# A projection of 2048 rows as eight units of seven products, with the sums of its operand's rows made on GpSimd

## The chip, the cores and the metric

One core of a Trainium2 chip runs the kernel. TensorE (PE) does matmuls, VectorE (DVE), ScalarE (ACT) and GpSimd (POOL) the elementwise work, and SyncE (SP) issues nearly all DMAs, in order, on one queue. The metric is the device time of one execution, in microseconds. Before the change it is 2262.46 us, the median of three runs (2262.41, 2262.46 and 2264.36).

## The reference

A decoder block on x of 1024 rows (time) and 1024 columns, in float32. Two mixers read the same normalised rows; a gated sum of their projections goes through an output projection and a squared-ReLU MLP. The part around the change:

```
o_a: 1024 x 512    (attention: four head slots of 128)
o_r: 1024 x 2048   (retention: four heads of 512; per head a recurrence over
                    chunks of 128 rows, group norm, scale and shift, times silu(gr))
y   = sigmoid(gate_a) * (o_a @ w_proj_a) + sigmoid(gate_b) * (o_r @ w_proj_b)
x   = x + y @ w_out
xn2 = rmsnorm(x, norm2_g)
x   = x + square(relu(xn2 @ w_up)) @ w_down
```

w_proj_b has 2048 rows and 1024 columns.

## The kernel before

**Numbers and layouts.** Each float32 operand is split into a high part h and a low part l (`split`, L318: ACT makes h in L319, DVE makes l = x - h in L320), and each product of two tiles is three matmuls, h h, h l and l h (`Pipe.group`). Operands are kept transposed: 128 columns of x or y on the partitions, the 1024 rows along the free axis, in two halves of 512 (`halves`, `cs`).

**Weights.** `Weights` (L38) holds the list of all weight loads and splits in the order of use. A raw buffer of 128 x 1024 is loaded by SP as soon as the buffer is free, and split into one of a few numbered buffers as soon as the products that read that buffer are done (`free`, `pump`). `add` (L61 on) takes a plain weight, `add_units` (L95) a unit of seven products: from two raw buffers it makes the pieces A, B and C (1024 columns each) and D (512), with four sums of 512 columns on DVE (L121) between them.

**Seven products.** `product` (L369) multiplies a 2 x 2 block matrix with seven products in place of eight: a unit is 256 output columns (f = 0, 1) by two halves of rows (lo, hi) over 1024 terms, and each product N1 to N7 has four terms of 128, so 12 matmuls. Its operands are sums and differences of the four quarters of the transposed input, made once and read by all units. Three PSUM banks and some copies put the products together, and `result(j, f, cs, src)` gets each of the four results. `in` (690 to 1002 us), `up` and `down` are made so in the kernel before; retention's output projection isn't.

**The order on the engines.** The order of the matmuls is written out by hand (`Pipe.step`, with functions set by `pipe.at` to come some steps later, such as retention's transposes), and a scheduler orders the other engines by the program's order and the waits. SP's DMAs form one queue, in which a DMA that waits holds up all behind it.

**Retention** (1002 to 1300 us). Per head h (4) and chunk c (8): values, scores, output and state on PE, the norm on DVE with the power on POOL (L853), then `turn_o` (L871): four transposes, scale and shift on ACT, the multiplication by the gate sr on DVE (L882), and one store of 4 x 128 rows by 128 columns to on_d in DRAM (L883).

**Projection of A** (1300 to 1360 us). For each block d of 128 output columns (8) and each half: 12 matmuls into a bank `ms`, then DVE multiplies by the gate sigmoid(gate_a) that was loaded from sg_d (L941), and the result is stored to pa_d. Beside it run the loads of the first half of o_r (`load_o`, 8 tiles of 128 x 1024 from on_d, each split). The first four go to buffers that are free already, the last four to buffers that are made when retention has ended.

**Projection of B** (1360 to 1534 us, L954 to L991). Two passes over w_proj_b's rows, first heads 0 and 1, then heads 2 and 3. Each pass is 8 blocks d x 2 halves of 8 terms x 3 = 24 matmuls (`project`, L959): 768 in all. In the first pass ACT copies the bank and SP stores it to pb_d, and the second half of o_r is loaded and split. In the second pass the sum of the first (pb_d), the gate (sg_d) and pa_d are loaded one step ahead, and DVE adds (L989), multiplies (L990), adds (L991), and the result is split into X, the operand of the next stage.

**Out** (1534 to 1640 us): y @ w_out in two halves of columns, 8 row tiles each, the residual, the norm and the transposes into the operands of `up` (OP7, six or seven sums of rows made on DVE).

## Time and profile before

| what | value |
|---|---|
| median of three runs | 2262.46 us |
| profiled execution, span | 2267.2 us |
| retention | 1002 to 1300.5 us |
| projection of A | 1301 to 1360.16 us |
| projection of B | 1360.16 to 1534.4 us |
| out | 1534.4 to 1640 us |
| HBM read, written | 200.48 MB, 92.37 MB |

The profiled execution is one of its own; its span, from the first to the last instruction on the core, stands in the second row. Times of stages are read from the first and last matmul or DVE instruction of the stage in the timeline. In the views, a row of windows has the stretch, its length, the busy time of each engine with its count of instructions, the granted clock of TensorE, the mean busy share of the 16 DMA engines and what they moved in GB/s. A row of groups has the line, engine, operation, output and inputs, shape and count, then the busy time in us, the mean ns of one, and the idle time before them with what ended it. A row of the timeline has start, duration and instruction, with what it waited for in brackets. A row of DMA issues has destination and source, queue, count, KB of each and the median us from issue to landing.

### The profile page before, as it was taken

Reading aid. Unit: us, or ns where it says so; the run is one execution under the profiler, and the core shown is the slowest. Engines: PE = TensorE matmul, PEld = TensorE weight load, DVE = VectorE, ACT = ScalarE, POOL = GpSimd, SP = SyncE. Lnnn points to the kernel's source line nnn. Section 1 sums busy time; section 2 is a strip of 40 time slices with the busy share of each in tenths; the row PEclk is TensorE's granted clock in tenths of the full one; section 3 lists DMA queues with packets and bytes.
Section 4 is the critical chain, followed back from the end, with each engine's and each line's share of the span. In section 5 each row is a group of like instructions: output and inputs, shape, how many; then the busy total and the mean of one; then the engine's idle time right before and its main releaser. Section 6 shows DMA issues by size and latency. Waiting matters only on the chain. (4 is left out here: it accounts for less than half of the span.)

```text
span 2267.2 us, 30458 instructions
## 1 busy us (share of the span) xinstructions
PE 2233.0 (98%) x10868; PEld 1912.0 (84%) x10868; DVE 1285.7 (57%) x2468; ACT 1014.0 (45%) x2294; POOL 344.3 (15%) x372
## 2 busy tenths in 40 slices
PE   8999999999999999999999999999999999899999
PEld 7999999998888888888888878888788888788777
DVE  6444545455544445558676753253855556687874
ACT  5444434345433333345555633112555545654542
POOL 1111111110000000000000000000000000587873
PEclk9999999999999999999999999999999999999999
DMA  4313232323233333363433385554345556645432
GB/s 148 98 52 105 65 91 85 94 85 99 82 109 106 110 109 111 113 186 117 122 117 97 121 267 183 155 184 153 107 127 151 151 152 199 218 153 179 169 129 102
DMA packets 227146, 294.85 MB, mean 130 GB/s; under 512 B 14129, under 2 KB 157873, under 8 KB 226994
## 3 DMA queue, kind: packets, MB, share of 16 engines
q1 hardware_dynamic: 226994, 292.91, 41.1%
q8 instruction: 85, 1.39, 0.3%
q14 instruction: 67, 0.55, 0.1%
HBM read 200.48 MB, written 92.37 MB: 129 GB/s over the span
## 5 line engine op out<-in xcount | busy, mean ns | idle before, releaser
L320 DVE TENSOR_TENSOR wl<-raw,wh 128x1024 fp32r<-128x1024 f32 (+2 forms) x274 | 300.4, 1099 | 398.0 <-ACT wh L319 396.9
L223 PE MATMUL mm<-wh,xh 128*128 128x384 f32 (+1 forms) x1226 | 482.0, 393 | 0.6 <-DVE Y L1203 0.5
L223 PE MATMUL mm<-wh,xl 128*128 128x384 f32 (+1 forms) x1226 | 438.8, 358 | 2.2 <-DVE xl L320 2.2
L223 PE MATMUL mm<-wl,xh 128*128 128x384 f32 (+1 forms) x1226 | 437.7, 357 | 0.0
L319 ACT ACTIVATE wh<-raw 128x1024 fp32r<-128x1024 f32 (+2 forms) x274 | 260.0, 951 | 358.2 <-PE ms L223 102.2
L223 PE MATMUL mm<-xl,wh 128*128 128x512 f32 x848 | 309.3, 389 | 1.7 <-DVE xl L320 1.7
L223 PE MATMUL mm<-xh,wh 128*128 128x512 f32 x848 | 309.7, 390 | 0.9 <-ACT ms L388 0.9
L223 PE MATMUL mm<-xh,wl 128*128 128x512 f32 x720 | 280.1, 389 | 0.0
L223 PEld LDWEIGHTS mm<-wh,xl 128*128 128x128 f32 x1226 | 230.9, 188 | 22.2 <-DVE xl L320 3.0
L223 PEld LDWEIGHTS mm<-wh,xh 128*128 128x128 f32 x1226 | 231.8, 189 | 20.0 <-DVE Y L1203 1.3
L223 PEld LDWEIGHTS mm<-wl,xh 128*128 128x128 f32 x1226 | 232.7, 190 | 16.6
L223 PE MATMUL ms<-xh,wh 128*128 128x512 f32 x604 | 239.3, 396 | 5.0 <-DVE s L941 3.5
L223 PE MATMUL ms<-xl,wh 128*128 128x512 f32 x604 | 235.8, 390 | 0.7 <-DVE xl L320 0.7
L223 PE MATMUL ms<-xh,wl 128*128 128x512 f32 x604 | 235.9, 391 | 0.0
L223 PEld LDWEIGHTS mm<-xl,wh 128*128 128x128 f32 x848 | 159.2, 188 | 34.9 <-DVE xl L320 2.1
L223 PEld LDWEIGHTS mm<-xh,wh 128*128 128x128 f32 x848 | 159.2, 188 | 34.2 <-ACT ms L388 1.3
L223 PEld LDWEIGHTS mm<-xh,wl 128*128 128x128 f32 x720 | 135.1, 188 | 28.1
L853 POOL TENSOR_TENSOR st<-st,half 128x1 f32<-128x1 f32 x32 | 25.8, 808 | 765.3 <-DVE st L852 765.3
L223 PEld LDWEIGHTS ms<-xh,wh 128*128 128x128 f32 x604 | 113.9, 189 | 31.2 <-issue 2.3
L223 PEld LDWEIGHTS ms<-xh,wl 128*128 128x128 f32 x604 | 113.7, 188 | 23.9
L223 PEld LDWEIGHTS ms<-xl,wh 128*128 128x128 f32 x604 | 113.9, 189 | 23.5 <-DVE xl L320 1.0
L333 POOL TENSOR_TENSOR ssa<-ssa,half 128x2 f32<-128x2 f32 x96 | 66.5, 693 | 427.9 <-DVE ssa L332 411.2
(296 smaller groups left out, 3605.1 us busy)
## 6 DMA issues: line engine op xcount, KB each, us to landing
raw<-in_w_att SPq DMA_DIRECT2D x48, 384.0 KB, 3.9
raw<-in_w_up SPq DMA_DIRECT2D x32, 512.0 KB, 3.9
h_d<-s SPq DMA_DIRECT2D x64, 256.0 KB, 4.5
raw<-in_w_down SPq DMA_DIRECT2D x32, 512.0 KB, 4.1
xh<-h_d SPq DMA_DIRECT2D x11, 896.0 KB, 4.5
xl<-h_d SPq DMA_DIRECT2D x10, 896.0 KB, 4.6
r<-h_d SPq DMA_DIRECT2D x10, 896.0 KB, 5.6
sg_d<-sg SPq DMA_DIRECT2D x32, 256.0 KB, 2.0
```

Source lines behind the costliest of these rows:

```text
L223: self.nc.tensor.matmul(ps, x, y, start=start, stop=stop, skip_group_check=not first)
L319: nc.scalar.activation(dst_h, src, AF.Copy)
L320: nc.vector.tensor_tensor(dst_l, src, dst_h.bitcast(F), op=OP.subtract)
L333: nc.gpsimd.tensor_tensor(dst, dst, half[:, :w], op=OP.pow)
L853: nc.gpsimd.tensor_tensor(st[:, 9:10], st[:, 8:9], half[:, 0:1], op=OP.pow)
```

## The change

Projection of B becomes eight units of seven products. w_proj_b is handed to `add_units` in quarters; units j = 0 to 3 are heads 0 and 1 (rows 0 to 1023 of w_proj_b), j = 4 to 7 heads 2 and 3. 8 units x 7 products x 12 matmuls are 672 matmuls.

The sums of rows that the seven products read are made in retention: a chunk c < 4 keeps its onT in one of five buffers and stores it; chunk c + 4 makes, on GpSimd, four sums and differences of 128 x 256 with it and stores ten row blocks (three DMAs) in place of four (one). on_d has 14 blocks for a head and a pair of chunks where it had 8. `load_sum` loads an operand's half, 128 x 1024, and splits it: 28 loads in place of 16, 12 of them beside the projection of A (after retention has made room, but for the first four, N5 and N7, whose buffers are there), four behind it, 12 in units 1 to 3, each operand of heads 2 and 3 one product after the last use of its buffer.

The gate is multiplied in both halves of the rows of w_proj_b: for each result the gate and an old sum (pa_d, or pb_d for j > 3) are loaded two results ahead, into rings of three buffers. DVE multiplies gate and product, which frees the bank; GpSimd adds the old sum (DVE for j = 7); for j < 4 the sum is stored to pb_d, for j > 3 it is split into the operand of out. The (f = 0, lo) results of j > 3 go through a small DRAM tile yl_d, since their place is still read. The buffers that w_out's weights are split into, and the places of out's and up's operands, change with it.

The diff, without places that only follow from it:

```diff
@@ -289,7 +289,8 @@
     sg_d = dram.tile([2, KT, P, S], F, name="sg_d")
     rqk_d = dram.tile([RH, 2, 2, P, S], F, name="rqk_d")
     sr_d = dram.tile([NF, P, S], F, name="sr_d")
-    on_d = dram.tile([NF, P, S], F, name="on_d")
+    on_d = dram.tile([RH, 14, P, 512], F, name="on_d")
+    yl_d = dram.tile([4, P, 512], F, name="yl_d")
     pa_d = dram.tile([KT, P, S], F, name="pa_d")
     pb_d = dram.tile([KT, P, S], F, name="pb_d")
     v_d = dram.tile([HEADS, S, DH], F, name="v_d")
@@ -352,12 +353,10 @@
             W.add(a["w_rv"][h, u])
     for d in range(KT):
         W.add(a["w_pa"][d])
-    for c in range(2):
-        for d in range(KT):
-            W.add(a["w_pb"][c, d])
+    W.add_units("pb", [a["w_pb_q"][j] for j in range(8)])
     for nb in range(2):
         for u in range(4):
-            W.add(a["w_out"][nb, u], (4, 5, 2, 3)[u] if nb else (2, 3, 0, 1)[u])
+            W.add(a["w_out"][nb, u], (4, 3, 2, 5)[u] if nb else (2, 5, 0, 1)[u])
     NU, RING = FF // 256, 10
     W.add_units("up", [a["w_up"][j] for j in range(NU)])
     NC = FF // 512
@@ -807,7 +806,7 @@
             gC = math.exp(C * math.log(1.0 - 2.0 ** (-5.0 - h)))
             us = W.take(4) if h else first
             St = cp.tile([P, 2, DV], F, name="St")
-            state = {}
+            state, firsts = {}, {}
             for c in range(NT):
                 ts = slice(c * P, (c + 1) * P)
                 load_chunk(NT * h + c + 2)
@@ -870,17 +869,34 @@
                     for f in range(2):
                         split(state["h"][:, f, :], state["l"][:, f, :], St[:, f, :])
 
-                def turn_o(c=c, h=h, ts=ts, it=it, sr=sr):
+                def put_sums(h, c, row, x):
+                    cut = slice((c % 4) * P, (c % 4 + 1) * P)
+                    nc.sync.dma_start(on_d[h, row:row + x.shape[1], :, cut].rearrange("f p t -> p f t"), x)
+
+                def turn_o(c=c, h=h, it=it, sr=sr, firsts=firsts):
                     pt = tr.tile([P, 4, P], F, name="tr")
                     for f in range(4):
                         nc.tensor.transpose(pt[:, f, :], it["o"][:, f * P:(f + 1) * P], ident)
-                    onT = p2.tile([P, 4, P], F, name="onT")
+                    early = c < NT // 2
+                    onT = p2.tile([P, 4, P], F, name="onE" if early else "onT", bufs=5 if early else 2)
                     for f in range(4):
                         fi = 4 * h + f
                         nc.scalar.activation(onT[:, f], pt[:, f], AF.Identity, scale=gng[:, 0, fi:fi + 1],
                                              bias=gng[:, 1, fi:fi + 1])
                     nc.vector.tensor_tensor(onT, onT, sr, op=OP.mult)
-                    nc.sync.dma_start(on_d[4 * h:4 * h + 4, :, ts].rearrange("f p t -> p f t"), onT)
+                    if early:
+                        firsts[c] = onT
+                        put_sums(h, c, 0, onT)
+                        return
+                    e, lo, hi = firsts[c - NT // 2], slice(0, 2), slice(2, 4)
+                    n6 = p2.tile([P, 2, P], F, name="n6")
+                    nc.gpsimd.tensor_tensor(e[:, lo], e[:, lo], onT[:, lo], op=OP.subtract)
+                    nc.gpsimd.tensor_tensor(n6, onT[:, hi], e[:, lo], op=OP.add)
+                    nc.gpsimd.tensor_tensor(e[:, hi], e[:, hi], n6, op=OP.subtract)
+                    nc.gpsimd.tensor_tensor(onT[:, lo], onT[:, lo], onT[:, hi], op=OP.subtract)
+                    put_sums(h, c, 4, e)
+                    put_sums(h, c, 8, onT)
+                    put_sums(h, c, 12, n6)
 
                 if h == c == 0:
                     pm = start
@@ -902,31 +918,31 @@
                     load_oa(c - 4)
 
 
-    before = XS[0, 0], XS[1, 0]
-    oS = [x for i in range(2) for x in as_rows(XS[i, 1])]
+    SUMS = ("N1", "N2", "N5", "N4", "N7", "N3", "N6")
     with ExitStack() as ph:
+        pr = pool(ph, "pr", 2)
         load = ExitStack()
         pm2 = pool(load, "pm2", 4)
 
-        pl = pool(load, "pl", 2)
-
-        def load_o(places, n):
-
-            for place in places:
-                raw = pl.tile([P, S], F, name="oraw")
-                nc.sync.dma_start(raw, on_d[n])
-                split(place[:, 0], place[:, 1], raw)
-                n += 1
-
-        def loaded(from_, src, name):
-            t = from_.tile([P, 512], F, name=name)
+        def loaded(from_, src, name, **kw):
+            t = from_.tile([P, 512], F, name=name, **kw)
             nc.sync.dma_start(t, src)
             return t
 
         ES, e1, exts = None, ExitStack(), ExitStack()
         work = [(d, cs) for d in range(KT) for cs in halves()]
         gates = [loaded(pm2, sg_d[0, d, :, cs], "s0") for d, cs in work[:3]]
-        waiting = [(place, n) for n, place in enumerate(oS)]
+        OPB = [{"N5": XS[0, 1], "N7": XS[1, 1]}, {}]
+
+        def load_sum(c, name, h):
+
+            raw = pr.tile([P, 2, 512], F, name="oraw")
+            o = 2 * SUMS.index(name)
+            nc.sync.dma_start(raw, on_d[2 * c + h, o:o + 2].rearrange("k p t -> p k t"))
+            xh, xl = OPB[c][name]
+            split(xh[:, 2 * h:2 * h + 2], xl[:, 2 * h:2 * h + 2], raw)
+
+        waiting = [(name, h) for name in ("N5", "N7", "N1", "N2", "N6", "N4") for h in range(2)]
         for d in range(KT):
             ua, = W.take(1)
             uh, ul = W[ua]
@@ -943,59 +959,92 @@
                 if ES is None and not pipe.due:
                     ret.close()
                     more = pool(body, "more", 1, "right")
+                    W.more = more
                     ext = pool(exts, "ext", 3, "right")
                     ES = [slot_of(ext) for _ in range(3)] + [slot_of(pool(e1, "ext1", 1, "right"))]
-                    waiting += [(place, 4 + n) for n, place in enumerate(as_rows(ES[0]) + as_rows(ES[1]))]
-                if waiting:
-                    place, n = waiting.pop(0)
-                    load_o([place], n)
+                    OPB[0].update({"N1": ES[0], "N2": ES[1], "N6": ES[3], "N4": ES[2], "N3": XS[0, 0]})
+                    OPB[1].update({"N1": XS[1, 0], "N2": ES[0], "N6": ES[1], "N5": ES[3], "N7": XS[0, 1],
+                                   "N4": XS[1, 1], "N3": ES[2]})
+                if waiting and (ES or waiting[0][0] in OPB[0]):
+                    load_sum(0, *waiting.pop(0))
         assert not waiting
-        other = places + as_rows(ES[2]) + as_rows(ES[3])
-        O = [oS + as_rows(ES[0]) + as_rows(ES[1]), other]
-        XS[0, 0], XS[1, 0] = ES[0], ES[1]
-
-        def project(c, d, cs, ub):
-            pp = mm.tile([P, 512], F, name="mm")
-            wh, wl = W[ub]
-            pipe.step(pp, [(wh[:, k * P:(k + 1) * P], wl[:, k * P:(k + 1) * P], O[c][k][:, 0, cs], O[c][k][:, 1, cs])
-                           for k in range(KT)], {KT - 1: lambda: W.free(ub)} if cs.start else None)
-            return pp
-
...
         load.close()
-        pm3 = pool(ph, "pm3", 2)
-
-        work = work[:-4] + [work[i] for i in (-4, -2, -3, -1)]
-        ubs = W.take(KT)
+        YS = [XS[0, 0], XS[1, 0], ES[0], ES[1]]
+        for h in range(2):
+            load_sum(0, "N3", h)
+            load_sum(1, "N1", h)
+
+        pub = pool(ph, "pub", 1)
+
+        class parts:
+            @staticmethod
+            def tile(shape, dtype, name):
+                return pub.tile(shape, dtype, name=name, bufs=2 if name == "u2" else 1)
+
+        pm3 = pool(ph, "pm3", 3)
+        order = [(0, "N1"), (1, "N1"), (0, "N2"), (1, "N2")]
+        for j in range(8):
+            more_n = [(j + 2, name) for name in ("N1", "N2")] if j < 6 else []
+            order += [(j, "N6"), (j, "N5"), *more_n[:1], (j, "N7"), *more_n[1:]]
+            order += [(j, name) for name in (("N4", "N3") if j < 6 else ("N3", "N4"))]
+        results = [(j, *{"N2": (0, 0), "N7": (1, 1), "N4": (1, 0), "N3": (0, 1)}[name])
+                   for j, name in order if name in ("N2", "N7", "N4", "N3")]
+        ahead, late = {}, {}
 
         def fetch(n):
...
+
+            if n >= len(results):
+                return
+            j, f, i = results[n]
+            d, cs = 2 * (j % 4) + f, halves()[i]
+            src = pa_d if j < 4 else pb_d
+            ahead[results[n]] = loaded(pm3, sg_d[1, d, :, cs], "s1"), loaded(pm3, src[d, :, cs], "s2")
+
+        def keep(j, f, cs, y):
+
+            yh, yl = (x[:, f, cs] for x in as_rows(YS[j - 4]))
+            split(yh, yl, y)
+
+        def result(j, f, cs, src):
+
+            n = results.index((j, f, cs.start // 512))
+            fetch(n + 2)
+            sgb, y = ahead.pop(results[n])
+            nc.vector.tensor_tensor(sgb, sgb, src, op=OP.mult)
+            if j < 4:
+                nc.gpsimd.tensor_tensor(y, y, sgb, op=OP.add)
+                nc.sync.dma_start(pb_d[2 * j + f, :, cs], y)
+            elif f or cs.start:
+                (nc.vector if j == 7 else nc.gpsimd).tensor_tensor(y, y, sgb, op=OP.add)
+                keep(j, f, cs, y)
+            else:
+                nc.gpsimd.tensor_tensor(y, y, sgb, op=OP.add)
+                nc.sync.dma_start(yl_d[j - 4], y)
+
+        after = {(3, "N1"): ("N2",), (3, "N2"): ("N6",), (3, "N6"): ("N5",), (3, "N5"): ("N7",), (3, "N7"): ("N4",),
+                 (3, "N4"): ("N3",)}
+        free = {(3, "N3"): 4, (7, "N1"): 5, (7, "N2"): 6, (7, "N6"): 7}
+        fetched = {order[order.index(at) - 3]: u for at, u in free.items()}
+        todo, unit = [], {}
+        fetch(0)
+        fetch(1)
+        for j, name in order:
+            product("pb", j, name, unit, OPB[j // 4], lambda: parts, result)
+            todo += [(new, h) for new in after.get((j, name), ()) for h in range(2)]
+            if todo:
+                load_sum(1, *todo.pop(0))
+            if (j, name) in free:
+                u = free[j, name]
+                lo, _ = halves()
+                keep(u, 0, lo, late.pop(u))
+            if (j, name) in fetched:
+                u = fetched[j, name]
+                late[u] = loaded(pm3, yl_d[u - 4], "s1")
+        assert not todo and not late
         e1.close()
 
 
-    W.more = more
-    OP7 = {"N1": before[0], "N2": before[1], "N3": XS[1, 1], "N5": XS[0, 1], "N4": XS[1, 0], "N7": XS[0, 0],
-           "N6": ES[2]}
+    OP7 = {"N1": XS[0, 1], "N2": XS[1, 1], "N6": ES[2], "N3": YS[0], "N5": YS[1], "N7": YS[2], "N4": YS[3]}
     norm2 = ExitStack()
     with ExitStack() as ph:
         cp = pool(norm2, "cp5", 1)
...
@@ -1336,8 +1385,8 @@
         "w_gate": np.stack([_blocks(w, gates[d], 4) for d in range(3)]),
         "w_gate_q": _quarters(w[:, np.concatenate(gates[3:])]),
         "w_pa": np.stack([_blocks(np.asarray(w_proj_a)[0], r(d * P, P), 4)[0] for d in range(KT)]),
-        "w_pb": np.stack([np.stack([_blocks(np.asarray(w_proj_b)[0][1024 * c:1024 * c + 1024], r(d * P, P), 8)[0]
-                                    for d in range(KT)]) for c in range(2)]),
+        "w_pb_q": np.concatenate([_quarters(np.asarray(w_proj_b)[0][np.concatenate(
+            [r(P * (8 * c + t), P) for t in (0, 1, 4, 5, 2, 3, 6, 7)])]) for c in range(2)]),
         "w_out": np.stack([_blocks(np.asarray(w_out)[0], r(nb * 512, 512), 2) for nb in range(2)]),
         "w_up": _quarters(np.asarray(w_up)[0]),
         "w_down": _down_quarters(np.asarray(w_down)[0]),
```

23 lines of the change are left out of this document (1 added, 22 removed).

## The prediction

> **What bounds the kernel now.** I read the page's busy shares, the cores, then windows of single stages, where PE's share says which engine sets the end.
>
> ```profile
> PE 2233.0 (98%) x10868; PEld 1912.0 (84%) x10868; DVE 1285.7 (57%) x2468; ACT 1014.0 (45%) x2294; POOL 344.3 (15%) x372
> ```
>
> ```profile
> core 0: 2267.2 us, clock 0.998
> ```
>
> ```profile
> core 0: us, PE busy (x) PEld busy (x) DVE busy (x) ACT busy (x) POOL busy (x), PEclk, DMA share, GB/s
> 691.36:862.69 171.33, 171.33 (x758) 141.86 (x757) 75.60 (x92) 58.39 (x84) 0.00 (x0) 1.00 0.34 111
> 1360.16:1534.40 174.24, 174.24 (x770) 144.30 (x769) 68.98 (x85) 41.75 (x55) 0.00 (x0) 1.00 0.54 173
> ```
>
> ```profile
> 1002.00:1300.50 298.50, 297.85 (x1449) 247.00 (x1448) 219.45 (x505) 162.46 (x342) 24.21 (x29) 1.00 0.41 122
> 1300.50:1367.50 67.00, 62.05 (x270) 49.55 (x269) 38.09 (x59) 23.43 (x37) 1.64 (x3) 0.97 0.85 272
> ```
>
> PE is busy 98% at clock 0.998: TensorE work sets the time. The second window of the first table is the old projection, from its first matmul to its last: 174.24 us, PE busy all of them, so 768 matmuls by the code at 0.227 each, no wait. The first is nine units of seven products in the input projection (84 matmuls each, between two copies of N1): 171.33 / 756 = 0.2267 us, also without a gap, so 19.04 us a unit and 2.72 a product of 12. Retention has no gap worth taking. The projection of A (1300.5 to 1360) is different: 5 us of PE are missing and DMA share is 0.85.
>
> **The change part by part**
>
> *Matmuls.* 8 units x 84 = 672 in place of 768: 96 x 0.2267 = **-21.8 us**, taken where PE had no gap. All else is whether the new stage keeps PE fed.
>
> *Sums in retention.*
>
> ```profile
> L1170 POOL TENSOR_TENSOR xl<-xl,xh x43: 727/739/2899, 1939.0 to 2244.6; 128x256 fp32r<-128x256 f32 x43
> ```
>
> ```profile
> 1275.46 0.69 DVE L882 TENSOR_TENSOR onT<-onT,sr 128x512 f32<-128x512 f32 x1
> ...
> 1280.15 0.89 POOL L853 TENSOR_TENSOR st<-st,half 128x1 f32<-128x1 f32 x1 [8.77 <-DVE st L852]
> ...
> 1281.81 0.54 DVE L855 TENSOR_SCALAR on<-on,st 128x512 f32<-128x512 f32 x1
> ```
>
> ```profile
> 1283.12 0.60 PE L876 MATMUL tr<-ident,on 128*128 128x128 f32 x4
> ```
>
> Each of the 16 chunks of a second half puts four sums of 128x256 on POOL. The nearest row is the down stage's: median 0.739, so 2.96; the longest single one took 2.9. They start when the gate multiplication ends (1276.15 in the chunk shown), end about 1279.1, and POOL's power for the norm (L853) is queued behind them; it started at 1280.15, and behind it stand DVE's L855 and PE's transposes, which began 0.8 us after L855 ended (1282.35 to 1283.12). So the sums fit by 1 us. If one took 2.9, the chunk is 1.2 late, less 0.8 slack. With three chunks of four at the median and the fourth with one long sum, four chunks would be 0.4 late each. SP's stores (three in place of one) wait for POOL too, and the loads of rq and sr, issued chunks ahead, queue behind them. No row shows either wait: bounds 0 and +3 (eight such chunks); I take **+0.5**, near the median's 0.
>
> By the Trainium skill, "SBUF — State Buffer", "Who interferes with whom", a DVE operation with two SBUF inputs and a GpSimd one that reads SBUF block each other for the whole instruction.
>
> ```profile
> L320 DVE TENSOR_TENSOR wl<-raw,wh 128x1024 fp32r<-128x1024 f32 x181 | 224.0, 1239 | 298.3 <-ACT wh L319 298.1
> ```
>
> ```profile
> L320 DVE TENSOR_TENSOR xl<-raw,xh 128x1024 fp32r<-128x1024 f32 x16 | 22.5, 1409 | 2.7 <-ACT xh L319 2.7
> ```
>
> The trace agrees as far as the split of 1024 columns takes 1.24 without POOL beside it and 1.41 in a group of the down stage, and POOL's sum goes from 0.73 to 2.9. By it a sum could lose up to 1.2 to one split in each chunk, which is inside the +3.
>
> *Projection of A.*
>
> ```profile
> 1328.00:1336.00 8.00, 8.00 (x37) 6.64 (x36) 4.49 (x6) 1.83 (x2) 0.00 (x0) 1.00 0.99 313
> 1336.00:1344.00 8.00, 7.56 (x33) 5.60 (x31) 2.15 (x3) 1.24 (x2) 0.00 (x0) 1.00 0.93 287
> 1344.00:1352.00 8.00, 5.79 (x24) 4.35 (x24) 5.67 (x6) 3.83 (x4) 0.00 (x0) 1.00 0.94 333
> 1352.00:1360.00 8.00, 7.01 (x24) 5.62 (x25) 3.85 (x6) 0.00 (x0) 0.00 (x0) 0.79 0.92 301
> 1360.00:1368.00 8.00, 8.00 (x37) 6.64 (x36) 2.11 (x3) 2.05 (x3) 0.00 (x0) 1.00 0.92 307
> ```
>
> ```profile
> PE ms L223 <- DVE s L941: 3.5, 2, 1.9
> ```
>
> ```profile
> DVE s L941 <- DMA s<-sg_d: 11.0, 6, 3.8
> ```
>
> ```profile
> 1312.03 0.68 DVE L320 TENSOR_TENSOR Sl<-St,Sh 128x512 fp32r<-128x512 f32 x1
> ```
>
> Here the DMA engines are already full: 0.92 to 0.99 busy at a mean of 308 GB/s. Gates land late, DVE's multiplication L941 waits for them, and PE for the bank, 3.5 us. After: 12 loads of sums of 512 KB, of which the first can start when the last split of the state has ended, 1312.7 (8 before, half of them earlier), and 16 gate loads. Up to the 13th gate 12.3 MB are queued from 1312.7; at 308 GB/s that is 40 us, 1353, + 4.3 to land + 0.7 + the last step of 2.7 = 1361 against 1360.2. I take **+1.2** (0 to 5; the end E = 1361.4).
>
> *Entry.* The first B and C can only be split when the last step of A has freed their buffers, one raw weight at a time. Unit 0's B is split by ACT and DVE (1.06 + 1.24, rows here and above), that frees a raw buffer, the next raw weight lands 4.6 later (next table), ACT splits it, and DVE then has the splits of A of unit 2, B of unit 1 and the first sum's N3 (3 x 1.24), 1.4 of smaller ones, and the first gate multiplication, 0.7: E+13.8. That multiplication frees the bank that unit 0's N5, the sixth product, needs at E + 5 x 2.72 = 13.6. **+0.5** (0 to 4, one more landing).
>
> ```profile
> L319 ACT ACTIVATE wh<-raw 128x1024 fp32r<-128x1024 f32 x181 | 191.4, 1058 | 297.5 <-PE ms L223 66.5 <-DMA raw<-in_w_up 56.3 <-PE mm L223 44.5
> ```
>
> *Loads of the new stage.*
>
> ```profile
> oraw<-on_d SPq DMA_DIRECT2D x16, 512.0 KB, 4.8
> ...
> raw<-in_w_pb SPq DMA_DIRECT2D x16, 512.0 KB, 4.6
> ```
>
> ```profile
> s<-sg_d SPq DMA_DIRECT2D x32, 256.0 KB, 3.3
> ...
> pa_d<-s SPq DMA_DIRECT2D x16, 256.0 KB, 4.3
> ...
> s<-pa_d SPq DMA_DIRECT2D x16, 256.0 KB, 3.7
> ```
>
> ```profile
> pb_d<-s SPq DMA_DIRECT2D x16, 256.0 KB, 2.1
> ```
>
> ```profile
> GB/s 148 98 52 105 65 91 85 94 85 99 82 109 106 110 109 111 113 186 117 122 117 97 121 267 183 155 184 153 107 127 151 151 152 199 218 153 179 169 129 102
> ```
>
> All is on one queue, in order. From 1312.7 to the second half's N3, the last operand: 28 loads of sums 14.7 MB, 13 weights 6.8, 32 gates 8.4, 20 of pa and pb 5.2, 16 stores of pa 4.2, 18 of pb and y 4.7, the rest of retention's stores 1.3, one reload 0.3: 45.6 MB. Then 4.8 to land and two splits, 2.3: 7.1. It is wanted at product 38, E + 103.4 = 1464.8. At 308 GB/s it is there at 1467.9 (+3), at 292 +11, at 287 (the slowest slice above) +14, at 333 (the fastest) it is early, and at 267, the page's best slice of 56.7 us, +26. I take 300, between the mean of the five full slices (308) and that of the two of lowest rate (294): by the code a load of a sum comes in rows of 2 KB where the old one had 4 KB, which no row prices. 45.6 / 0.300 = 152 us, + 7.1 = 1471.8, **+7** (0 to +26). Were the DMA engines free, the loads, each issued a product after the one before it from unit 3's N1 on, would land and be split by E+98.5, in time; so the rate decides.
>
> The Trainium skill ("DMA: Bandwidth & Descriptors", "Where 436 GB/s comes from") gives about 358 GB/s for HBM to SBUF, and by it the 45.6 MB take an estimated 127 us and this term is 0; the trace's full slices stay at 287 to 333.
>
> *DVE and POOL in a unit.*
>
> ```profile
> L121 DVE TENSOR_TENSOR raw<-raw,raw 128x512 f32<-128x512 f32 x74 | 51.9, 702 | 1.9
> ```
>
> DVE was busy 75.60 / 9 = 8.4 a unit in the input projection. Added are four gate multiplications (2.8) and in units 1 to 3 four splits of sums (5.0): 16.2 of 19.04. POOL, idle in this stage, gets four additions of 128x512, an estimated 1.48 each (two of 0.74): 5.9. No term, as long as DVE's margin of 2.8 isn't taken.
>
> *Exit.*
>
> ```profile
> L320 DVE TENSOR_TENSOR xl<-s,xh 128x512 fp32r<-128x512 f32 x16 | 11.1, 693 | 11.2 <-ACT xh L319 11.2
> ```
>
> ```profile
> 862.69 0.58 ACT L388 ACTIVATE ms<-mm 128x512 f32<-128x512 f32 x1
> ```
>
> After unit 7's last product come a multiplication and an addition on DVE (1.4), and two keeps of 0.58 on ACT and 0.69 on DVE (2.5). In ACT's and DVE's order a split of w_out's second half (2.3) stands ahead of the last two keeps, and its raw weight is asked for late. 6.2 with the weight there, up to 9.8 if its landing (4.6) is wholly in the way; out's first tile needs the rows after 21 matmuls, 4.8. So 1.4 to 5 late, 0 if the scheduler's neighbours run otherwise: **+2.5**. The second pass's adds (L989 and on) go, at no price: PE never waited for them.
>
> *Sum.* -21.8 + 0.5 + 1.2 + 0.5 + 7 + 2.5 = **-10.1**. The profiled execution's span, 2267.2, is 4.7 above the median of the runs, 2262.46; I take the difference as it is: 2262.5 - 10.1 = **2252.4**.
>
> **The rivals.** *Transfers hidden* (333 GB/s or more, or bytes needed earlier than I count): the +7 is gone: 2262.5 - 21.8 + 0.5 + 1.2 + 0.5 = 2243, with the exit's 2.5 2245. For it: the slice at 333. Against: five slices average 308. *DMA-bound, gain eaten:* 287 to 267 GB/s, +14 to +26 in place of +7: 2259 to 2271, no change or a little slower. For it: slices at 287 and 267.
>
> *Slower: the ring of y buffers.* Each result loads its old sum into one of three buffers, POOL adds, the buffer is stored, and the load three results later waits for that store on the queue that also brings weights and sums.
>
> ```profile
> DMA to landing us min/median/max: 3.0/3.7/7.0
> ```
>
> ```profile
> DMA to landing us min/median/max: 2.8/4.1/7.1
> ```
>
> These are on_d's and pa_d's landings. Load + multiplication 0.69 + addition 1.48 + store must fit three results, 3 x 4.76 = 14.3. With medians it is 10. With the longest, 7.1 + 0.69 + 1.48 + 7.0 = 16.3, plus 0.35 for the queue, 16.6, 5.54 a result; 32 x 5.54 = 177 against 152: +25 in place of the +7: 2270.5. It decides from 16.3 us a ring (half of that loss by 15.3). Medians speak against it; full DMA engines in the first 100 us speak for.
>
> **How the numbers follow.** Forecast 0.45 (own range 2246 to 2258); hidden 0.15; DMA-bound 0.20; ring 0.20. A measurement tells about 0.2% (4.5 us) from no change. Faster (under 2258): the first two and a small part of the third, 0.62; same: 0.16 of the third and 0.02 of the ring (half of its loss); slower: 0.18 of the ring and the third's far end, 0.02. Range: 2243, all hidden, to 2270, ring or 267 GB/s.
>
> **What would show it.** The new stage's window from E: 152.3 us and 672 matmuls if fed. PE idle at product 38 until the split of a sum's load shows the bytes. PE idle until a gate multiplication frees its bank, with DVE waiting for a gate's or y's landing, shows the ring; the same at the sixth product alone, the entry; PE idle at out's first tile, the exit. POOL's sums in retention longer than 0.74 and PE idle at the transposes would show the port. Wrong would make it a gap at a place that I did not price, for one DVE late in units 1 to 3, or a unit not of 19.04 us.

## The result, and the profile after

The change made the kernel slower: 2282.14 us against 2263.01 of before, median of four runs each; ratio 1.0084, 95% interval 1.0070 to 1.0098. Forecast were 2252.4 and a range that ended at 2270.

The profiled execution of the change spans 2279.2 us, 12.0 more than that of before. The medians are 19.1 apart: the profile of before is of a long execution (its span alone is 4 us above the median of its runs), so some 7 us of the loss can't be placed by stage. Page and cores:

```profile
PE 2222.4 (98%) x10772; PEld 1898.7 (83%) x10772; DVE 1349.3 (59%) x2531; ACT 1044.1 (46%) x2330; POOL 444.8 (20%) x465
```

```profile
core 0: 2279.2 us, clock 0.992
```

PE has the 96 matmuls less in its count and yet a lower clock, 0.992 after 0.998. The windows of the change, from the end of retention to the first matmul of the new stage, and from there to the first matmul of out; columns as before:

```profile
1300.50:1367.73 67.23, 57.90 (x242) 45.67 (x240) 39.15 (x60) 24.96 (x39) 13.35 (x16) 0.92 0.81 253
1367.73:1547.61 179.88, 161.68 (x673) 130.65 (x672) 129.64 (x147) 70.25 (x90) 48.08 (x29) 0.94 0.75 252
```

The same boundaries were 1360.16 and 1534.2 before. So, from profile to profile, retention and the projection of A together end 7.6 us later (1.0 of it in retention, read at the scores of a head's last chunks, 1281.35 after 1280.37), and the new stage takes 179.9 us where its matmuls need 152.3 and the old one took 174.1: 672 matmuls keep PE busy for 161.7 us, 9.4 of them from a slower clock, and 18.2 us are idle. From out on the two are the same within 1.4 us. The waits of PE in the new stage (line, what it waited for, us in total, times, longest):

```profile
PE mm L223 <- ACT ms L387: 8.5, 3, 7.0
PE mm L223 <- DVE u L396: 7.3, 2, 4.5
PE mm L223 <- DVE s L1013: 2.1, 1, 2.1
PE ms L223 <- ACT u L395: 0.3, 1, 0.3
```

The old stage had no wait at all. Three places make up 16.4 of the 18.2: the first gate multiplication (L1013, 2.1), a copy of N1 (L387, 7.0, between products of unit 3), and the last two units (L396, 4.5 and 2.8). The timeline of ACT around the second:

```profile
1448.81 1.05 ACT L320 ACTIVATE xh<-oraw 128x1024 fp32r<-128x1024 f32 x1
1458.21 1.06 ACT L320 ACTIVATE xh<-oraw 128x1024 fp32r<-128x1024 f32 x1 [8.35 <-DMA oraw<-on_d]
1459.17 0.58 ACT L387 ACTIVATE ms<-mm 128x512 f32<-128x512 f32 x1
```

The split of a sum whose load had not landed stands ahead of the copy that frees PE's bank: ACT waits 8.35 us with nothing to do, PE 7.0. Each longer wait costs a second time. PE after the shortest of the three, by the timeline:

```profile
1386.31 0.48 PE L223 MATMUL mm<-xh,wh 128*128 128x512 f32 x1 [2.10 <-DVE s L1013]
1386.61 0.59 PE L223 MATMUL mm<-xl,wh 128*128 128x512 f32 x1
1387.01 0.63 PE L223 MATMUL mm<-xh,wl 128*128 128x512 f32 x1
...
1389.99 0.42 PE L223 MATMUL mm<-xh,wh 128*128 128x512 f32 x1
1390.26 0.39 PE L223 MATMUL mm<-xl,wh 128*128 128x512 f32 x1
```

For some 3.4 us the matmuls come 0.43 us apart in place of 0.227: after 2.1 us of idle another 1.7 us are lost. The Trainium skill ("TensorE: Matmul & The Clock Gate", "Part 1: The HAM clock gate") has a half clock for about 3.4 us after an idle window of that length; here 2.1 us of idle were enough. Not every such wait costs it: in the profiles of all kernels here but e2, from 1300 to 1560 us, PE's waits of up to 1.65 us were followed by none of the slow matmuls, all those of 2.84 us or more were, with 1.4 to 3.0 us lost, and those between (1.78 to 2.83) in some places were and in others weren't (2.33 us in e4 and 2.83 in e14 cost nothing).

### The profile page after: what moved, and what is told of

It is laid out like the page before. It is cut to its first block, busy times and chain, and to the rows that moved or that the text cites. A ratio compares the mean times of both kernels' runs of the same rounds, so it can differ in the third digit from the quotient of the medians.

```text
span 2279.2 us, 30618 instructions
## 1 busy us (share of the span) xinstructions
PE 2222.4 (98%) x10772; PEld 1898.7 (83%) x10772; DVE 1349.3 (59%) x2531; ACT 1044.1 (46%) x2330; POOL 444.8 (20%) x465
## 5 line engine op out<-in xcount | busy, mean ns | idle before, releaser
L321 DVE TENSOR_TENSOR wl<-raw,wh 128x1024 fp32r<-128x1024 f32 (+2 forms) x290 | 321.6, 1112 | 361.5 <-ACT wh L320 360.6
L223 PE MATMUL mm<-xh,wh 128*128 128x512 f32 x720 | 284.3, 395 | 18.0 <-ACT ms L387 8.5
L223 PE MATMUL ms<-xh,wh 128*128 128x512 f32 x700 | 277.8, 397 | 9.8 <-DVE s L957 9.2
L223 PE MATMUL mm<-xl,wh 128*128 128x512 f32 x720 | 283.1, 393 | 1.7 <-DVE xl L321 1.7
L223 PE MATMUL ms<-xl,wh 128*128 128x512 f32 x700 | 274.0, 391 | 0.7 <-DVE xl L321 0.7
L223 PE MATMUL ms<-xh,wl 128*128 128x512 f32 x700 | 273.9, 391 | 0.0
L223 PEld LDWEIGHTS mm<-xh,wh 128*128 128x128 f32 x720 | 136.8, 190 | 49.5 <-ACT ms L387 10.0
L223 PEld LDWEIGHTS ms<-xh,wh 128*128 128x128 f32 x700 | 132.6, 189 | 41.0 <-DVE s L957 8.3
L223 PEld LDWEIGHTS mm<-xl,wh 128*128 128x128 f32 x720 | 136.9, 190 | 30.4 <-DVE xl L321 2.1
L223 PEld LDWEIGHTS ms<-xl,wh 128*128 128x128 f32 x700 | 132.4, 189 | 27.5 <-DVE xl L321 1.0
```

The costliest lines, as they stand in the source:

```text
L223: self.nc.tensor.matmul(ps, x, y, start=start, stop=stop, skip_group_check=not first)
L321: nc.vector.tensor_tensor(dst_l, src, dst_h.bitcast(F), op=OP.subtract)
```

## The experiments

All are compared with runs of the kernel before on the same chip; its medians there were 2265.1 to 2266.3, where it was 2263.0 beside the change. A ratio is always to these. The runs went in six groups (the change, e1 to e4, e5 to e8, e9 to e12, e13 to e15, e16 to e18). e8 and e11 turned out to have the same order of instructions on every engine and are 3.3 us apart, in two groups: so much is scatter, and differences of 2 or 3 us between groups say nothing. The theories are those of the expectations: Q (a wait holds all that stands behind it in its engine's order), B (bytes on the DMA engines), E (DVE and GpSimd too busy, or locking each other out). The first and last matmul of the new stage are read from PE's timeline in each profile, as above; the table gathers what the sections use.

| run | median, us | new stage from | its length, us |
|---|---|---|---|
| change | 2282.1 | 1367.7 | 179.9 |
| e1 sums alone, old projection | 2277.8 | 1367.5 | 174.1 |
| e2 stores issued by GpSimd | 2364.2 | | |
| e3 late splits | 2293.0 | 1366.9 | 193.1 |
| e4 additions on DVE | 2280.5 | 1369.6 | 178.3 |
| e5 order of the last units | 2280.1 | 1365.3 | 180.3 |
| e6 eight gate buffers | 2277.8 | 1356.5 | 187.4 |
| e7 12 sum loads left out | 2284.6 | 1369.4 | 181.9 |
| e8 three edits (e4, e5, e6) | 2263.7 | 1357.6 | 170.9 |
| e9 kernel before, eight gate buffers | 2261.8 | 1353.9 | 174.1 |
| e10 last sums on DVE | 2281.6 | 1367.9 | 181.8 |
| e11 as e8, gates first in the text | 2260.5 | 1355.8 | 170.3 |
| e12 as e11, splits one product later | 2260.8 | 1356.3 | 170.2 |
| e13 loads ahead | 2266.3 | 1358.0 | 172.8 |
| e14 as e13, additions on GpSimd | 2277.0 | 1360.6 | 184.9 |
| e15 as e13, four gate buffers | 2267.5 | 1368.9 | 168.4 |
| e16 as e11, four old-sum buffers | 2260.1 | 1355.4 | 168.7 |
| e17 as e11, 12 loads left out | 2255.9 | 1356.3 | 166.0 |
| e18 as e11, 16 stores left out | 2254.9 | 1355.3 | 166.7 |

### Where the projection of A loses 7 us: e1, e10, e6, e9

e1 is the kernel before with turn_o and put_sums of the change and on_d of 14 blocks; only the loads' source follows:

```diff
-                nc.sync.dma_start(raw, on_d[n])
+                nc.sync.dma_start(raw.rearrange("p (k t) -> p k t", k=2),
+                                  on_d[n // 4, 2 * (n % 4):2 * (n % 4) + 2].rearrange("k p t -> p k t"))
```

> The old projection of two passes with the new retention: GpSimd makes the sums and stores all 14 row blocks, and the old 16 loads read blocks of these, so what is projected is not o. It is the cost of the sums alone. Theory Q (queues: a waiting DMA or split holds up all that stands behind it in its engine's order): stores of the last two chunks make SP wait for GpSimd while the projection of A needs its gates, so that stage ends 3 to 6 us late; with 1 us of retention 2267 to 2270. Theory B (bytes: DMA engines full): 1.3 MB more of stores in that stage, 4 us at 300 GB/s at most, half of it hidden: 2264 to 2266. Theory E (DVE and GpSimd too busy, or locking each other out): only retention's 1 us: 2264.

2277.8, ratio 1.0056 (1.0041 to 1.0072), more than any theory gave: 12 us by the medians; in the profiles the stage behind starts 7.3 us later and is as long as before. More than half of the loss is there without any new product.

e10 makes head 3's last sums on DVE:

```diff
+                    eng = nc.vector if h == RH - 1 and c >= NT - 2 else nc.gpsimd
-                    nc.gpsimd.tensor_tensor(e[:, lo], e[:, lo], onT[:, lo], op=OP.subtract)
+                    eng.tensor_tensor(e[:, lo], e[:, lo], onT[:, lo], op=OP.subtract)
...
```

> The change, with the eight sums of head 3's chunks 6 and 7, which fall into the projection of A, made on DVE. Theory Q, waits for GpSimd (its sums of 0.7 to 1.7 us hold the sums' stores, these hold the stores of results, and these the gates): -4 to -8, 2274 to 2278. Theory B or a ring that is too small anyway: -2 to +1.

2281.6, nothing. It took away only a part: SP's waits for GpSimd's sums in the projection of A are 7.1 us after 13.3, and 5.4 us of waits for DVE's onT have come up. e6 widens the ring of gates:

```diff
-        pm2 = pool(load, "pm2", 4)
+        pm2 = pool(load, "pm2", 8)
-        gates = [loaded(pm2, sg_d[0, d, :, cs], "s0") for d, cs in work[:3]]
+        gates = [loaded(pm2, sg_d[0, d, :, cs], "s0") for d, cs in work[:6]]
```

> The change, with eight buffers for the gates in the projection of A in place of four, and six loaded ahead in place of three. Theory Q in that stage (a gate's load waits until the product of four results before has been stored, and that store stands behind the sums' stores that wait for GpSimd): the stage's stalls of 9 us go with their slow clock: -6 to -10, 2271 to 2275. Theory B: the same bytes, the gates come earlier but sums' loads later: -3 to +2, 2278 to 2283.

2277.8, and the new stage starts at 1356.5, 11.2 us earlier, with no wait over 0.84 us left in the projection of A, though SP still waits 14.3 us for GpSimd's sums there. With the same bytes: the ring of four paced it. SP's timeline in the change, and its longest sum of waits in that stage:

```profile
1334.83 0.45 SPq L958 DMA_DIRECT2D pa_d<-s  x1
1335.33 0.44 SPq L941 DMA_DIRECT2D oraw<-on_d  x1
1335.86 0.46 SPq L958 DMA_DIRECT2D pa_d<-s  x1
1340.41 0.32 SPq L929 DMA_DIRECT2D s<-sg_d  x1
```

```profile
SPq L929 <- DMA pa_d<-s: 23.7, 11, 5.1
```

A gate's load waits until the result of four steps before has been stored and landed, and SP stands still meanwhile. A store to pa_d lands after 5.4 us by the median where it took 4.3 before, and SP's waits for GpSimd's sums are new; which of the two makes the ring's turn longer in the change isn't told apart. The kernel before has the same ring, and SP waited for it as much:

```profile
SPq L923 <- DMA pa_d<-s: 24.5, 12, 4.8
```

e9 is e6's edit on it:

> The kernel before, with eight gate buffers in the projection of A and six loaded ahead, as in the run of that edit on the change. If the ring of four paces that stage in the kernel before too (3.5 us of waits and a slow clock): -4 to -7, 2258 to 2261. If its loads' bytes do: 2264 to 2266.

2261.8, ratio 0.9987 (0.9978 to 0.9997): 3.6 us faster, and all waits of that stage are gone:

```profile
1300.50:1353.85 53.35, 53.22 (x243) 43.66 (x241) 38.46 (x59) 24.60 (x38) 1.65 (x3) 1.00 0.84 295
1353.85:1527.93 174.08, 174.08 (x770) 144.21 (x768) 69.01 (x84) 41.97 (x54) 0.00 (x0) 1.00 0.55 181
```

The 48 us from 1312 on in the kernel before, in the change and in e9 show that the DMA engines' rate wasn't used up there:

```profile
1312.00:1360.00 48.00, 44.36 (x190) 35.45 (x189) 25.05 (x35) 13.86 (x20) 0.55 (x1) 0.96 0.86 277
1312.00:1360.00 48.00, 39.03 (x158) 30.66 (x157) 23.27 (x30) 14.96 (x21) 9.37 (x9) 0.89 0.85 268
1312.00:1360.00 48.00, 48.00 (x217) 39.68 (x216) 31.25 (x40) 19.69 (x26) 0.55 (x1) 1.00 0.97 348
```

### What lengthens the new stage: e4, e5, e7, e3, e2

e4 puts the 32 additions of old sums on DVE (three times `nc.gpsimd.tensor_tensor(y, y, sgb, op=OP.add)` becomes `nc.vector...`).

> The change, with all 32 additions of old sums on DVE, none on GpSimd. Theory Q: a store waits 0.7 us for DVE in place of 1.3 to 2.2 for GpSimd, and the keeps come earlier: 2272 to 2279. Theory B: 2280 to 2282. Theory E, if DVE's time is what lacks (2.8 us more per unit of 19): 2285 to 2295; if it is the lock between the two: 2268 to 2275, as the sums of 1.67 us on DVE beside GpSimd go back to 0.7.

2280.5, 1.7 less, which the scatter covers. The groups of the change, and of e4, in the new stage:

```profile
L1015 POOL TENSOR_TENSOR s<-s,s 128x512 f32<-128x512 f32 x16 | 27.8, 1750 | 113.7 <-DVE s L1013 96.4 <-DMA oraw<-on_d 10.1 <-DMA s<-pa_d 7.1
```

```profile
L321 DVE TENSOR_TENSOR wl<-raw,wh 128x1024 fp32r<-128x1024 f32 x26 | 34.4, 1334 | 9.9 <-ACT wh L320 9.8
L121 DVE TENSOR_TENSOR raw<-raw,raw 128x512 f32<-128x512 f32 x14 | 13.5, 964 | 0.2
```

```profile
L321 DVE TENSOR_TENSOR wl<-raw,wh 128x1024 fp32r<-128x1024 f32 x26 | 31.6, 1222 | 12.8 <-ACT wh L320 12.8
L121 DVE TENSOR_TENSOR raw<-raw,raw 128x512 f32<-128x512 f32 x15 | 10.2, 683 | 0.0
```

One addition on GpSimd takes 1.75 us where 1.48 were estimated, and DVE's sum of 512 takes 0.96 on the mean where it takes 0.68 without GpSimd (e4's rows are the last two). The mean hides two kinds: of the stage's 29 such sums six take 1.66 or 1.67 us, each with over 1.1 us of a GpSimd addition beside it, and 23 take 0.67 to 0.69. So the two hold each other up. SP's order is held up too, in the change:

```profile
SPq L1016 <- POOL s L1015: 22.7, 11, 4.9
SPq L929 <- POOL s L1018: 21.0, 8, 4.5
SPq L929 <- DMA pb_d<-s: 12.9, 9, 3.4
```

Its stores of results, and its loads into buffers that an addition still uses, wait 43.7 us for GpSimd. In e4 these waits are gone, those for pb_d are 34.4 us, and the time is hardly other; that any of this decided something isn't shown here. e5 changes the order of the last two units:

```diff
-            order += [(j, name) for name in (("N4", "N3") if j < 6 else ("N3", "N4"))]
...
+        order += [(6, "N6"), (6, "N5"), (6, "N7"), (7, "N6"), (6, "N4"), (6, "N3")]
+        order += [(7, "N5"), (7, "N7"), (7, "N4"), (7, "N3")]
```

> The change, with unit 7's N6 moved between unit 6's N7 and N4, and N4 ahead of N3 in both. In the change N3 stands right behind N7 there, with no product between, and adds to the bank that DVE has still to read. Theory T (order of the last units): the two gaps of 4.5 and 2.8 us there shrink to one of about 1, with their slow clock: -7 to -10, 2271 to 2275. Theory Q (queues) or B (bytes) alone: these gaps come from late splits and stay: 2279 to 2283.

2280.1, 2 less, within the scatter too. The 7.3 us of waits for L396 are gone as expected, and from the copy of unit 7's N1 to out it takes 42.8 us after 47.2; but the stage is as long as before, since the wait at the first gate multiplication was 3.9 in this run after 2.1, and others of 1.3 and 2.5 stand in the last units. e7 leaves 12 loads out:

```diff
+            if c and name != "N1":
+                raw = same["raw"]
+            else:
+                raw = same["raw"] = pr.tile([P, 2, 512], F, name="oraw")
...
```

> The change, where all operands of the second half but N1 are split from the tile that N1's second load brought, so 12 loads of 512 KB in units 1 to 3 are left out and their splits kept (the product isn't right then). Theory Q or B (the loads of sums are late, and ACT and DVE stand still for them): the gap of 7.0 and the smaller ones in units 1 to 3 go: -8 to -12, 2269 to 2273. Theory E (DVE and GpSimd too busy there): -2 at most: 2279 to 2282.

2284.6, nothing gained. The gap of 7.0 is gone, and waits of 1.8, 2.4, 1.5, 1.1 and 3.3 us stand in units 2 to 5, behind ACT's splits of weights and of results. So the late sum was only one of several things that were late, and the bytes of these loads, the forecast's term, weren't the bound in the change as made.

e3 loads each sum straight into its low part's place and splits it three products later:

```diff
-            raw = pr.tile([P, 2, 512], F, name="oraw")
-            nc.sync.dma_start(raw, on_d[2 * c + h, o:o + 2].rearrange("k p t -> p k t"))
+            nc.sync.dma_start(xl.bitcast(F), on_d[2 * c + h, o:o + 2].rearrange("k p t -> p k t"))
+            parting.append((pipe.slot + hold, xh, xl, xl.bitcast(F)))
...
```

> The change, with each sum loaded straight into its low part's place (no raw buffer), and the splits of the second half's sums put three products later in the program's order, still ahead of their first use. Theory Q: ACT's and DVE's orders no longer stand still for a load that is late, so the gap of 7.0 us and its slow clock go: 2271 to 2274. Theory B: PE waits for the operand itself some products later: 2279 to 2282. Theory E: the same work: 2281.

2293.0, 11 us slower than the change, by no theory: the new stage takes 193.1. Two edits are in it, and the load now needs the operand's place to be free, so which of them costs is not told apart. e2 issues GpSimd's stores from GpSimd (`nc.gpsimd.dma_start` in put_sums for c > 3 and in result):

> The change, with the stores of what GpSimd makes (the sums of chunks 4 to 7, the old sums to pb_d and yl_d) issued by GpSimd itself, behind its own operations, so SP's queue has no wait for GpSimd. Theory Q: the loads behind those stores come earlier, the gap of 5.7 us in the projection of A and that of 7.0 in the new stage go with their slow clock: 2266 to 2272. Theory B: the same bytes at the same rate: 2279 to 2283. Theory E: GpSimd gets more to do by issuing: 2281 to 2290.

2364.2, 82 us more; one such group of stores in retention, by GpSimd's timeline:

```profile
1066.78 0.92 POOL L874 DMA_DIRECT2D on_d<-onT  x1
1070.81 0.77 POOL L874 DMA_DIRECT2D on_d<-onE  x1 [3.10 <-issue]
1071.57 0.71 POOL L874 DMA_DIRECT2D on_d<-n  x1
1072.29 0.57 POOL L852 TENSOR_TENSOR st<-st,half 128x1 f32<-128x1 f32 x1
```

Three issues hold GpSimd 5.5 us, and the norm's power stands behind them, PE's transposes behind that (4.5 us here). It says nothing on the queue of SP.

### The edits together: e8, e11, e12

e8 is the edits of e4, e5 and e6 in one:

> The change with three edits together: additions of old sums on DVE, the last two units' order as with unit 7's N6 moved, eight gate buffers in the projection of A. If the parts add up (-1.7, -8, -8): 2261 to 2266, the time before or a little under. If the DMA engines' bytes are behind it all: 2276 to 2282.

2263.7, ratio 0.9997 (0.9987 to 1.0007) to before: 18.4 us less than the change, where the three alone gave 1.7, 2.1 and 4.3. Each taken against the kernel before in its own group, it is 20.9 where they gave 4.4, 4.6 and 6.9, so the three seem to give 5 to 10 us more together than one by one, which is likely but not sure with a scatter of some 3 us on each number. The traces show where the parts hinder each other: in e6 the new stage starts 11 us earlier and takes 7.5 longer, since what it starts with didn't come earlier by as much. The first gate multiplication begins at 1380.4 after 1385.5, and PE waits 6.6 us for it in place of 2.1. The last units need two of the edits: 47.2 us from the copy of unit 7's N1 to out in the change, 46.8 with additions on DVE, 42.8 with the order, 38.5 with both (e8). From unit 0's N1 to unit 7's, 111.5 us of matmuls, it takes 128.5 in the change and 128.9 in e8.

e11 also puts `fetch(0)` and `fetch(1)` ahead of the last four calls of `load_sum` before the loop, e12 besides holds each split of units 1 to 3 back by one product, as in e3 but from the raw buffer:

> The three edits of the run before (additions on DVE, order of the last units, eight gate buffers) and the first two gates and old sums of the new stage loaded ahead of the four last sums' loads, which wait for raw buffers. Theory Q: the gap of 5.6 us before the first gate multiplication goes with its slow clock: -5 to -8 against the three, 2256 to 2259. Theory B: the wait moves to the sums: 2262 to 2265.

> As the run of four edits, and each split of the second half's sums one product later in the program than its load. Theory Q: ACT no longer stands still 5.2 us for a load ahead of the copy of unit 3's N7, and the gap of 3.6 goes: -3 to -6 more, 2251 to 2256. Theory B, or if the load behind then waits for the raw buffer: 2256 to 2262.

2260.5 and 2260.8, ratios 0.9984 (0.9975 to 0.9993) and 0.9983 (0.9974 to 0.9992). e11 tells nothing of its edit: the scheduler put the loads back where they were, so it is e8 once more. PE still waits 5.8 us at the first gate multiplication. SP's timeline there, and what it waited for between 1364 and 1379:

```profile
1368.77 3.62 SPq L941 DMA_DIRECT2D oraw<-on_d  x2
1372.44 0.46 SPq L929 DMA_DIRECT2D s<-sg_d  x1
```

```profile
SPq L941 <- DVE xl L321: 8.0, 4, 2.3
```

The first row merges two issues, at 1368.77 and 1372.02. The gate's load stands behind two sums' loads that wait for a raw buffer. e12, in e11's group, made the gap of 4.0 in unit 3 one of 2.9 and gave no time.

### What still holds the new stage: e13 to e18

e13 keeps the additions on DVE and the order of the last units, has six gate buffers in the projection of A, gives the second gates a ring of their own, loads its first two early, and loads sums up to two ahead of their split:

```diff
+        pg = pool(ph, "pg", 3)
-        pm2 = pool(load, "pm2", 4)
+        pm2 = pool(load, "pm2", 6)
...
+            if d == KT - 2:
+                early = [loaded(pg, sg_d[1, i, :, halves()[0]], "s1") for i in (0, 2)]
...
-                load_sum(1, *todo.pop(0))
+                part_sum(1, *todo.pop(0))
+                if later:
+                    get_sum(1, *later.pop(0))
```

> Additions on DVE and the last units' order as before; the second gates get a ring of their own, with its first two loaded before the end of the projection of A (whose ring is six); the second half's sums are loaded up to two ahead of their splits, so a split finds its data landed. The bytes are the same. If the waits on late loads are the rest of the loss: the gaps of 5.8 and 4.0 go with their slow clock, -8 to -13 against the run of four edits, 2247 to 2253. If the DMA rate is: 2258 to 2264.

2266.3: wrong. The wait for the gate is gone, and waits of 4.6 us for a copy of N1 at the third product and of 4.0 in unit 3 are there. e14 and e15 undo one edit of e13 each:

> As the run with loads ahead, but the additions of old sums on GpSimd, as in the change. If GpSimd's slower additions and the longer DVE operations beside them cost by themselves: +6 to +15 against it. If only the late loads did: -2 to +3.

> As the run with loads ahead, but the projection of A with four gate buffers and three loaded ahead, as in the kernel before and in the change. If that ring paces its stage: +6 to +11 against it. If the new stage catches up what it lost there, since loads pace it: 0 to +4.

e14 takes 2277.0, so GpSimd's additions cost 10.7 us beside the other edits, in one group of runs; the stage is 12 us longer, with 22.8 us of waits on PE after 12.9. By what way isn't told apart: the longer operations on DVE, the slower addition itself, or SP, which waits 34.6 us for GpSimd in e14's new stage. e15 takes 2267.5, only 1.2 more by the medians (the two profiled executions are 7.0 apart): the stage starts 11 us later and is 4.4 shorter. e16 to e18 change the ring of old sums, the 12 loads, and the 16 stores to pb_d, from e11:

```diff
-            fetch(n + 2)
...
-            ahead[results[n]] = loaded(pm3, sg_d[1, d, :, cs], "s1"), loaded(pm3, src[d, :, cs], "s2")
+            ahead[results[n]] = loaded(pm3, sg_d[1, d, :, cs], "s1", bufs=2), loaded(pm3, src[d, :, cs], "s2", bufs=4)
...
+            fetch(n + 2)
```

```diff
-                nc.sync.dma_start(pb_d[2 * j + f, :, cs], y)
...
-            src = pa_d if j < 4 else pb_d
+            src = pa_d
```

> The run of four edits, with four buffers for old sums in place of three and two for the second gates, loaded behind the result's addition. A load of an old sum then waits for the store of two results before, not of the last. If the ring of old sums paces the stage: -5 to -12 against the run of four edits, 2249 to 2256. If bytes do, or the splits' latency: -2 to +4.

> The run of four edits, with the 12 loads of sums in units 1 to 3 left out (split from a tile loaded before; the product isn't right then). If bytes pace the stage (6.3 MB at some 285 GB/s are 22 us of the DMA engines): -8 to -14 against the run of four edits, 2247 to 2253. If the ring of old sums does: -3 to +1.

> The run of four edits, without the 16 stores of the first half's sums; the second half adds pa's product in their place (the product isn't right then). The old sums' ring then waits for no store in units 0 to 3. If the ring paces the stage: -6 to -12 against the run of four edits, 2249 to 2255. If bytes do, 4.2 MB of some 45: -3 to -8. If the latency of each split does: 0.

e16 takes 2260.1, 0.3 less than e11, the lowest of those that leave nothing out: ratio 0.9978 (0.9968 to 0.9987) to before. SP's wait for stores to pb_d is half of what it was, e11 first:

```profile
SPq L929 <- DMA pb_d<-s: 30.6, 15, 4.3
```

```profile
SPq L929 <- DMA pb_d<-s: 16.8, 12, 2.4
```

and the time hardly moves: not the ring. e17 and e18, which have e11's ring, are 4.3 and 5.3 below e16 in the same group, for 6.3 and 4.2 MB less; in e7 the first of these gave nothing. So once A's ring, the additions and the order are out of the way, these transfers cost some 5 us, by their bytes or by the waits for them; in both runs the stage still takes 166 to 167, of which 5.1 and 6.6 are the one wait at the first gate multiplication.

## Why the prediction was wrong, point by point

From profile to profile the time went up by 12.0 us where 10.1 less were forecast, 22.1 off. Of these 17.6 are in the new stage: above its matmuls the forecast had 10 us there (entry 0.5, loads 7, exit 2.5), and it took 27.6, 18.2 of waits and 9.4 of slow clock. 5.4 are in the projection of A. So the sum failed at A's bound and, by more, at what it put at nothing in the new stage: the order of the last units and the slow clock behind each wait, with additions on GpSimd behind a part of the waits.

- **Matmuls, -21.8: right.** 96 fewer, and 0.2267 each where PE doesn't wait.
- **Sums in retention, +0.5: right**, 1.0 in the profile.
- **Projection of A, +1.2: the step that failed first.** It took the DMA rate for the bound, as the engines were 0.92 to 0.99 busy there. Measured +6.6, and e6 and e9 took the waits away with all bytes left; in e9 the engines moved 348 GB/s where the forecast counted on 308. The bound is the ring of four gate buffers: load, multiplication, store. The row that said so was at hand, 11.0 us of DVE's waits for sg_d; the forecast read it as a full engine, not as a load that was issued late.
- **Entry, +0.5:** 2.1 of wait and 1.7 of slow clock. The wait for the first gate multiplication is there, at the seventh product and not the sixth, and that operation ends 18.4 us into the stage where 13.8 were summed; the gate for it landed only at 1385.45, behind two sums' loads. As soon as A is faster, 5 to 6.6 us stand there.
- **Loads of the new stage, +7: near in size, wrong in kind.** Unit 3's gap is 7.0 and other small waits 1.8, with the slow clock 12 or so. But it doesn't lie at product 38, and e7 shows that without the loads the time stays. That the number came near is luck.
- **DVE and POOL in a unit, no term: failed,** though DVE was hardly fuller than summed: from the copy of unit 2's N1 to that of unit 7's it is busy 13.6 to 17.2 us from one copy to the next, where 16.2 were counted. What the forecast left out is that the two wait for each other, 1.75 for 1.48 on GpSimd and some of DVE's sums 1.67 for 0.68, and that SP's queue waits for GpSimd. Alone it can't be told from scatter (e4), with other waits removed it is 10.7 (e14). The rule on the shared port from the Trainium skill ("SBUF — State Buffer", "Who interferes with whom"), which the forecast weighed for retention alone, fits the six longer sums; that it alone made the 10.7 isn't shown.
- **Exit, +2.5:** not seen (and its upper end of 9.8 doesn't follow from its parts: 6.2 and 4.6 are 10.8). In its place stands a wait that the forecast had no term for: N3 right behind N7 in the last two units, 4.5 and 2.8 us and their slow clock, some 10 in all.
- **The slow clock** after each wait, 9.4 us in the stage, had no term; the row of before that showed it (0.79 in 1352 to 1360) stood in the forecast.
- **The rivals.** The slower one had the sign. With additions on DVE its mechanism, the ring of old sums, isn't the bound: e16 halves its wait on SP for 0.3 us. In the change as made GpSimd's additions are a part of that ring's turn and SP waits 56.6 us for them and for pb_d; no run widens the ring there, so it stays possible as the way by which these additions cost time. The DMA-bound one is a part, some 5 us beside e16 (e17, e18), and not of the change as made (e7).

Shown are A's ring, the price of GpSimd's additions beside the other edits, and the waits that the order of the last units made. Open is by what way the additions cost. Open is also what paces the first five units and the entry when those are gone: e13 moved its waits, and no run took them all away. Also open is the cost in e3, and why e15 loses so little.

## What to carry to other kernels

A stage that fed PE without a wait has slack that no row names: before a change puts splits, loads and stores beside it, follow each in-order queue (ACT, DVE, SP) and ask what stands behind a wait, since waits removed one at a time gave 2 to 7 us here, little more than scatter, and three together 18 to 21. A DMA share near 1 doesn't prove that bytes are the bound; a ring of buffers that is load, use and store deep looks the same, and one run with a wider ring tells. And compare with the best form of the old code: two constants in e9 brought the kernel before to 0.9987 of its time, and the new stage with all its edits is at 0.9978 (e16), with intervals that overlap.

## What the runs showed of the hardware

- After 2.1 us without work PE took 8 matmuls at 0.43 us in place of 0.227; after 1.16 us none. Over all runs but e2 the price begins at waits of 1.8 us and is certain only from 2.84 us on, where it is 1.4 to 3.0 us besides the wait itself.
- DVE's sums of 128x512 take 0.67 to 0.69 us, or 1.66 to 1.67 with most of a GpSimd addition beside them, in the change; the GpSimd additions of that shape take 1.27 to 2.28.
- Three stores issued by GpSimd took it 5.5 us in retention (e2); SP takes 0.46 us for each by the median (the change).
- In e11 the DMA engines moved more in 8 us than any row of before showed (a transfer counts where it starts, so the share can pass 1):

```profile
1320.00:1328.00 8.00, 8.00 (x39) 6.58 (x38) 4.56 (x7) 4.29 (x10) 3.55 (x5) 1.00 1.06 394
```
